# Low weight parts by ScalarE and an accumulating DMA in place of a VectorE subtraction: a decoder layer in split fp32 on one core

## The chip, the cores and the metric

The kernel runs on one core of one Trainium2 chip. The metric is the device time of one execution in microseconds (us). Five engines work side by side, each through its own queue in order: TensorE (PE in the profile, PEld its weight loads), VectorE (DVE), ScalarE (ACT), GpSimd (POOL) and SyncE (SP). SP issues nearly all DMAs of this kernel; 16 DMA engines carry them.

## The reference

One step of a decoder trunk with one layer, for a prompt of 1024 tokens and 8 sample tokens (1032 columns in all), width 1024, everything in fp32:

```
h   = rms_norm(x);  q, k, v, u, gates = split(h @ w_in)            # w_in: 1024 x 6400
a   = attention(q, k, v) @ w_attn_out                              # 3 groups of 4 heads, windows 128/512/2048
c   = swish(layer_norm(conv31(glu(u)))) @ w_conv_out
x  += rms_norm((sig(g0) * a + sig(g1) * c) @ w_out)
x  += rms_norm((silu(g) * up) @ w_ffn_out),  g, up = split(rms_norm(x) @ w_ffn_in)
x  += sigmoid(rms_norm(x) @ w_ple_gate) * (p @ w_ple_proj)
```

Besides x the kernel returns the new rows of the key/value caches and of the convolution's state.

## The kernel before

**Products in three passes.** Each fp32 operand is split into a high part in the type fp32r and a low part, the rest. A product of two split operands takes three matmuls: high by high, low activation by high weight, high activation by low weight. `mm3` issues them in this order; its three lines are L256, L257 and L258 in the profile. So L258 is the one that reads a weight's low part.

**Weights.** A weight tile is 128 partitions by 1024 fp32 (512 KB). `wq` lists 106 plain ones and 38 others in the order of use. `load_weight` loads a tile by a DMA on SP into one of `NRAW` = 3 buffers called `raw`. `ensure(i)` sees to it that the plain weights up to i are split: ScalarE copies `raw` into `wh` (high part, rounded to fp32r), VectorE subtracts, `wl = raw - wh`. The 38 weights of the first feed forward product from hidden tile 3 on go through `fetch` and `prepare` (Strassen's form, tiles `wah`, `wbh` ...) instead. `wh` and `wl` are slots of a pool of 43 that all large tiles share, so a new `wh` or `wl` may first wait until the last reader of its slot is done.

**Stages** (us of the profiled span): `w_in` with the depthwise convolution and the attention beside it, to about 520; branch gates with the combination of the attention groups and the layer norm of the convolution, to 690; the projection of branch A (`wi_A`), then of the convolution (`wi_C`, three weights held at a time), to 803; the output projection (`wi_O`, eight weights at once, by quarters of the tokens, `o_bank`), to about 895; the feed forward's first product (three plain hidden tiles, then Strassen's form), to 1355; its second product (`w_ffn_out`) in groups of hidden tiles, to 1609; the last gate (`wi_P`, `p_bank`) with the projection of p (`wi_pp`), to the end.

**Order.** The kernel is emitted in program order, but a scheduler moves instructions within each engine's queue by its own estimate of when each can run, except in `first_pairs`, where the order is pinned. A tile that is written or read in another way is thus not only produced differently: instructions around it on PE, ACT, DVE and POOL can change places too.

**GpSimd** before the change does 20 small powers, `r1 = r0 ** -0.5` in `token_rstd`, which give each norm's factors, and a few fills at the start. All engines' calls go through a wrapper, so that most lines of the profile on ACT, DVE and POOL read L116; one goes by the tiles' names.

Of the kernel before, what the change touches and what calls it, by code (L numbers as in the profile page):

```python
# [10 lines left out]
F32 = mybir.dt.float32  # L11
F32R = mybir.dt.float32r
AF = mybir.ActivationFunctionType
# [13 lines left out]
# token chunks; the last holds 256 prompt tokens and the 8 sample tokens  # L27
# [4 lines left out]
NRAW = 3  # L32
BUD = 2.95
# [3 lines left out]
# token chunks of the parts after the mix  # L37
# [17 lines left out]
def decoder_step(ctx: ExitStack, tc: tile.TileContext, ins, outs):  # L55
# [50 lines left out]
    class Engine:  # L106
        """An engine; its instructions stay in the order of emission while pinned[0] holds."""
# [59 lines left out]
    wq = []          # weight requests in the order of use: (dram view [128, n, 128], n)  # L167
# [21 lines left out]
    def fetch(j):  # L189
        """The next weight as it comes."""  # L190
        assert w_emitted[1] == j
        while w_emitted[0] < min(j + NRAW, len(wq)):
            load_weight()
        w_emitted[1] += 1
        return raws.pop(j)

    def ensure(i):
        """Weights up to i are loaded and split, the next ones on their way."""
        i = min(i, len(wq) - 1)
        while w_emitted[1] <= i:  # L200
            while w_emitted[0] < min(w_emitted[1] + NRAW, len(wq)):
                load_weight()
            j = w_emitted[1]
            r, n = raws.pop(j), wq[j][1]
            hi, lo = act("wh", F32R), act("wl", F32R)
            A.activation(hi[:, :n * P], r[:, :n * P], AF.Copy)
            V.tensor_sub(lo[:, :n * P], r[:, :n * P], hi[:, :n * P].bitcast(F32))
            wt[j] = tuple(x[:, :n * P].rearrange("p (k m) -> p k m", m=P) for x in (hi, lo))
            w_emitted[1] += 1
# [8 lines left out]
    def pump(us):  # L218
        """Background work of about so many microseconds of VectorE."""
        credit[0] += us  # L220
        while credit[0] > 0 and bg:
            try:
                credit[0] -= next(bg[0]) or 1.0
            except StopIteration:
                bg.popleft()
        if not bg:
            credit[0] = 0
# [3 lines left out]
    def tick(us):  # L231
        """Once per bank of `us` microseconds: the first chain goes on as far as VectorE's share allows."""
        if chains:
            ch = chains[0]
            ch[1] += us * RATE
            while ch[1] > 0:
                try:
                    ch[1] -= next(ch[0])
                except StopIteration:
                    chains.popleft()  # L240
                    break

    def finish(key):
        """The chains up to the one named."""
        while any(ch[2] == key for ch in chains):
            tick(5)
# [4 lines left out]
    def rng(c):  # L251
        """The token range of a chunk: its number among CH, or the range itself."""
# [7 lines left out]
    def gemm_bank(wi, xs, c, nk=KT, mid=None):  # L260
        """One bank: 128 output features by the tokens of chunk c."""
# [13 lines left out]
    def gemm_bank_rows(wis, f, xs, c):  # L275
        """One bank, the weights held by rows: wis[k] has all output features of k."""
# [19 lines left out]
    def token_rstd(acc, c):  # L296
        """acc: SBUF [128, chunk] -> rstd columns of the tokens from the sums over the partitions."""
# [22 lines left out]
    class SumSq:  # L320
        """Sum of squares over feature tiles."""
# [25 lines left out]
    def split_scaled(src, g, hi, lo, c):  # L347
        """src * g per feature -> hi and lo."""
# [5 lines left out]
    def chunk_slots(name):  # L354
        """Four slots that hold a chunk of eight feature tiles, and the tiles' views."""
# [9 lines left out]
    # =====================================================================  # L365
    # weight order
    # =====================================================================
# [19 lines left out]
    # feed forward: the first tiles as they are, then pairs of gate and up  # L387
# [13 lines left out]
    # =====================================================================  # L401
    # start: loads, transposes, first norm, pp = p @ w_ple_proj
    # =====================================================================
# [44 lines left out]
    def setup():  # L448
# [25 lines left out]
        # relative position biases: table values by distance, as rows for skewed reads and as columns  # L474
# [41 lines left out]
        # biases of the sample's slots: the first 13 by distance, the tokens' own in every 16th row  # L516
# [143 lines left out]
    def qkv_out(i):  # L660
        """The rows of the sample's tokens."""
# [12 lines left out]
    def kv_prompt_out(g, hp, dst, srcT):  # L674
        """The prompt's last rows, features by positions in the group's order."""
# [215 lines left out]
    # =====================================================================  # L891
    # phase 1: u / q, k, v with convolution and attention beside them
    # =====================================================================
# [56 lines left out]
    def first_pairs():  # L950
        """The first norm and the first two pairs, chunk by chunk.

        The products of the chunks 0 and 1 start before the factors of the tokens are known; they come in
        with the banks' results, and the chunks' operands are made again with them.
        """
# [86 lines left out]

# [27 lines left out]
    # branch gates  # L1070
# [12 lines left out]
    # =====================================================================  # L1083
    # branch A's projection; swish of the convolution; branch B; merge
    # =====================================================================
# [24 lines left out]
    def blocks(wis, fn, per, nc_=3):  # L1110
        """Blocks of `per` weight tiles held on chip, the chunks outermost inside a block."""
# [26 lines left out]
    def residual_norm(c, mv, rb, v_post, d_res, sq2, per):  # L1138
        """mv(f) (f32) -> residual + its norm in place, tile by tile; the sums of squares into sq2."""
# [13 lines left out]
    # =====================================================================  # L1153
    # output projection, by quarters of the tokens; norms up to the feed forward
    # =====================================================================
    # the mix as f32: halves of the tokens, two feature tiles to a slot
# [24 lines left out]
    # Strassen's form of the products with w_ffn_in (Winograd's variant): sums of the operands' quarters  # L1181
    tsum = [[None] * 4 for _ in range(2)]

    def token_sums(p):
        """The sums of the quarters of h2 for the tokens of half p: T1 = B12 - B11, T2 = B22 - T1,
        T3 = B22 - B12, T4 = B21 - T2, as hi and lo, four feature tiles to a slot."""
# [31 lines left out]
    def cache_copies():  # L1218
        """The caches move up by one row."""
# [13 lines left out]
    # =====================================================================  # L1233
    # feed forward, first product: hidden tiles into DRAM
    # =====================================================================
# [15 lines left out]
    def prepare(j):  # L1251
        """Gate's and up's weights of hidden tile j (A11, A12; A21, A22: tiles by halves of the features):
        S1 = A21 + A22, S2 = S1 - A11, S3 = A11 - A21, S4 = A12 - S2, as hi and lo."""
# [112 lines left out]
    # =====================================================================  # L1366
    # feed forward, second product, in groups of hidden tiles
    # =====================================================================
# [29 lines left out]
    # the last norm's operand, by chunks: three feature tiles to a slot  # L1398
    hp = [None] * 3

    def last_chain(ci, sq):
        """Residual and norm; the last norm's operand without the factors of the tokens, these into rbs."""
# [19 lines left out]
    for ci, c in enumerate(LC):  # L1422
# [7 lines left out]
        if nf < KT:  # L1430
            # the last banks side by side: the operands are done with one after the other
# [16 lines left out]
    # =====================================================================  # L1448
    # per-layer embedding gate and the outputs
    # =====================================================================  # L1450
# [87 lines left out]
def _lay_out(x):  # L1538
    """The inputs as the chip reads them: features by tokens, weights by tiles."""
# [17 lines left out]
def _rows(k, v, g):  # L1557
    """[2, 128 features, positions] of K and V -> [rows, 2, 4, 64] in the order of time."""
# [32 lines left out]
```

## Time and profile before

| | |
|---|---|
| Time, median of two runs | 1735.7 us (1734.86 to 1736.55) |
| Span of the profiled execution, first to last instruction | 1731.0 us |
| TensorE busy (matmul) | 1712.0 us, 99% |
| TensorE busy (weight loads) | 1661.9 us, 96% |
| VectorE busy | 1220.9 us, 71% |
| ScalarE busy | 620.9 us, 36% |
| GpSimd busy | 21.5 us, 1% |
| DMA | 171.47 MB, packets 29.8% of 16 engines' time on SP's queue |

The page gives the profiled execution's span and not a time of its own with what lies around the span; the two runs lie 3.9 to 5.6 us above that span, their median 4.7. A busy PE is one with a matmul in flight: matmuls overlap, so its share tells how little it idled, not how near it is to its peak.

### The profile page before, as it was taken

The page shows a single profiled execution, that of the slowest core. Times are in us where ns is not written, and L with a number is a line of the kernel's source. Part 1 is how long each engine was busy: PE and PEld are TensorE (multiplying, and loading weights), DVE is VectorE, ACT ScalarE, POOL GpSimd, SP SyncE. Part 2 cuts the span into 40 slices and gives each one's busy share as a digit, 9 for nine tenths or more (in the row PEclk, how much of TensorE's full clock was granted, in tenths as well). Part 3 has the DMA queues.
Part 4 walks back from the last instruction along what each step waited for, and adds up shares of the span by engine and source line. Part 5 has one row for each costly group of instructions (what it writes and reads, how often), then busy time and mean ns, then how long its engine had stood idle before and what let it go on. Part 6 is the DMA issues. An engine that isn't in the chain of part 4 may idle for free.

```text
span 1731.0 us, 29699 instructions
## 1 busy us (share of the span) xinstructions
PE 1712.0 (99%) x12086; PEld 1661.9 (96%) x12086; DVE 1220.9 (71%) x2188; ACT 620.9 (36%) x1303; POOL 21.5 (1%) x29
## 2 busy tenths in 40 slices
PE   7999999999999999999999999999999999999999
PEld 7999998999989999999999999999999999999998
DVE  7899779858969696744577866666666545637863
ACT  6434434444352254323354432233332311213530
POOL 0000000000000000000000000000000000000000
PEclk9999999999999999999999999999999999999999
DMA  5231121121343322622252232233333532520411
GB/s 188 65 121 65 43 66 44 60 75 41 112 156 103 123 95 96 203 80 85 80 163 70 74 98 94 86 98 98 110 98 116 188 138 90 181 94 13 148 58 45
DMA packets 82254, 171.47 MB, mean 99 GB/s; under 512 B 11026, under 2 KB 52034, under 8 KB 81734
## 3 DMA queue, kind: packets, MB, share of 16 engines
q1 hardware_dynamic: 82118, 169.58, 29.8%
q8 instruction: 94, 1.54, 0.4%
q14 instruction: 42, 0.34, 0.1%
HBM read 133.04 MB, written 50.01 MB: 106 GB/s over the span
## 4 chain that ended last, share of the span: by engine, by line
PE 96%; DVE 2%; issue 1%; POOL 0%; DMA 0%; ACT 0%; POOLq 0%; SPq 0%; DVEq 0%
PE g L256 30%; PE g L258 30%; PE g L257 30%; PE S L592 1%; PE O L630 1%; PE PT L615 1%; DVE ogl L116 1%; PE m L317 0%; PE m L300 0%; PE m L690 0%; POOL r L116 0%; DVE acc L116 0%; DMA raw<-in_w_in_dram 0%; PE m L876 0%; DVE cs L116 0%
## 5 line engine op out<-in xcount | busy, mean ns | idle before, releaser
L256 PE MATMUL g<-hh,wh 128*128 128x384 f32 (+1 forms) x1200 | 393.3, 328 | 7.0 <-ACT wh L116 7.0
L257 PE MATMUL g<-hl,wh 128*128 128x384 f32 (+1 forms) x1200 | 386.6, 322 | 0.0
L258 PE MATMUL g<-hh,wl 128*128 128x384 f32 (+1 forms) x1200 | 386.3, 322 | 0.3 <-DVE wl L116 0.3
L116 DVE SCALAR_TENSOR_TENSOR y<-z,taps,y 128x1023 f32<-128x1023 f32 (+14 forms) x240 | 304.2, 1267 | 31.7 <-ACT y L116 26.1
L256 PEld LDWEIGHTS g<-hh,wh 128*128 128x128 f32 x1200 | 227.2, 189 | 10.7 <-ACT wh L116 7.0
L258 PEld LDWEIGHTS g<-hh,wl 128*128 128x128 f32 x1200 | 226.8, 189 | 1.5 <-DVE wl L116 0.8
L257 PEld LDWEIGHTS g<-hl,wh 128*128 128x128 f32 x1200 | 227.3, 189 | 0.9
L257 PE MATMUL g<-ul,wh 128*128 128x344 f32 x528 | 168.9, 320 | 0.0
L258 PE MATMUL g<-uh,wl 128*128 128x344 f32 x528 | 168.7, 320 | 0.0
L256 PE MATMUL g<-uh,wh 128*128 128x344 f32 x528 | 162.8, 320 | 0.6 <-DVE fa L116 0.6
L116 DVE TENSOR_TENSOR wl<-raw,wh 128x1024 fp32r<-128x1024 f32 x106 | 128.9, 1220 | 22.9 <-ACT wh L116 19.9
L116 DVE TENSOR_TENSOR pk<-pk,g 128x258 f32<-128x258 f32 x266 | 105.3, 420 | 52.4 <-PE g L258 36.9
L256 PE MATMUL g<-mh,wh 128*128 128x258 f32 x448 | 127.2, 285 | 0.0
L258 PE MATMUL g<-mh,wl 128*128 128x258 f32 x448 | 126.6, 283 | 0.0
L257 PE MATMUL g<-ml,wh 128*128 128x258 f32 x448 | 126.5, 283 | 0.0
L116 ACT ACTIVATE wh<-raw 128x1024 fp32r<-128x1024 f32 x106 | 110.7, 1052 | 6.5 <-DMA raw<-in_w_in_dram 4.2
L116 DVE TENSOR_TENSOR fa<-fa,g 128x344 f32<-128x344 f32 x96 | 47.1, 511 | 76.9 <-PE g L258 76.5
L258 PEld LDWEIGHTS g<-uh,wl 128*128 128x128 f32 x528 | 99.2, 188 | 0.0
L257 PEld LDWEIGHTS g<-ul,wh 128*128 128x128 f32 x528 | 99.2, 188 | 0.0
L256 PEld LDWEIGHTS g<-uh,wh 128*128 128x128 f32 x528 | 98.1, 188 | 0.9 <-DVE fa L116 0.9
L256 PE MATMUL g<-th,wbh 128*128 128x258 f32 x304 | 86.0, 283 | 0.0
L258 PE MATMUL g<-mh,wal 128*128 128x258 f32 x304 | 86.0, 283 | 0.0
(246 smaller groups left out, 3840.3 us busy)
## 6 DMA issues: line engine op xcount, KB each, us to landing
raw<-in_w_in_dram SPq DMA_DIRECT2D x50, 512.0 KB
raw<-in_w_ffn_in_dram SPq DMA_DIRECT2D x44, 512.0 KB
hr<-d_h SPq DMA_DIRECT2D x22, 516.0 KB
raw<-in_w_ffn_out_dram SPq DMA_DIRECT2D x22, 512.0 KB
d_h<-pk SPq DMA_DIRECT2D x38, 258.0 KB
out_kvs_dram<-in_cache_kv_w_dram SPq DMA_DIRECT2D x16, 510.0 KB
res<-in_xT_dram SPq DMA_DIRECT2D x8, 516.0 KB
d_x<-mo SPq DMA_DIRECT2D x32, 129.0 KB
```

Of the source, the lines that this page charges most:

```text
L116: ins = fn(*a, **k)
L256: TE.matmul(ps, hi_w, xh, start=first, stop=False)
L257: TE.matmul(ps, hi_w, xl, start=False, stop=False)
L258: TE.matmul(ps, lo_w, xh, start=False, stop=last)
L592: TE.matmul(sp[h][:, ko:256], qT[h * 64:(h + 1) * 64, blk * P:(blk + 1) * P], kT[h * 64:(h + 1) * 64, k0:k0 + nk], start=True, stop=True)
L615: TE.transpose(ps[:, o:o + P], e[:, o:o + P], ident)
L630: TE.matmul(ps[h * 64:(h + 1) * 64, :P], vtok[:, (blk - 1 + kb) * P + h * 64:(blk - 1 + kb) * P + (h + 1) * 64], p[:, (h * 2 + kb) * P:(h ...
```

## The change

`ensure` makes the low part in another way for every plain weight but the first four. ScalarE writes the negated high part into `wl` (the same rounding, with a factor of -1), and a DMA issued from GpSimd adds `raw` to it in place. The subtraction on VectorE goes.

```
+FIRST = 4
 ...
     def ensure(i):
         ...
             r, n = raws.pop(j), wq[j][1]
             hi, lo = act("wh", F32R), act("wl", F32R)
             A.activation(hi[:, :n * P], r[:, :n * P], AF.Copy)
-            V.tensor_sub(lo[:, :n * P], r[:, :n * P], hi[:, :n * P].bitcast(F32))
+            if j < FIRST:
+                V.tensor_sub(lo[:, :n * P], r[:, :n * P], hi[:, :n * P].bitcast(F32))
+            else:
+                A.activation(lo[:, :n * P], r[:, :n * P], AF.Copy, scale=-1.0)
+                G.dma_start(lo[:, :n * P].bitcast(F32), r[:, :n * P], accum_op=ALU.add)
             wt[j] = tuple(x[:, :n * P].rearrange("p (k m) -> p k m", m=P) for x in (hi, lo))
```

Counted in the built programs: 102 subtractions leave VectorE, 102 passes of 128x1024 come to ScalarE, 102 DMAs of 512 KB to GpSimd's queue. Three places show how the queues stand. Lines shift with the change: L256 to L258 become L262 to L264.

**ScalarE at the start of the output projection**, before (`mo` is a bank's result, `sq` and `acc` its squares for the norm, `wh` the high part of the next weight):

```order
L116 ACTIVATE mo_7947<-g_7955 128x258
L116 ACTIVATE wh_7985<-raw_7745 128x1024
L116 ACTIVATE acc_7981<-mo_7947 128x258
L116 ACTIVATE wh_8020<-raw_7941 128x1024
L116 ACTIVATE mo_7947<-g_7989 128x258
L116 ACTIVATE sq_8015<-mo_7947 128x258
L116 ACTIVATE mo_7948<-g_8024 128x258
L116 ACTIVATE wh_8055<-raw_7983 128x1024
```

and now:

```order
L117 ACTIVATE mo_8005<-g_8013 128x258
L117 ACTIVATE wh_8043<-raw_7801 128x1024
L117 ACTIVATE acc_8039<-mo_8005 128x258
L117 ACTIVATE wl_8044<-raw_7801 128x1024
L117 ACTIVATE wh_8079<-raw_7998 128x1024
L117 ACTIVATE mo_8005<-g_8048 128x258
L117 ACTIVATE wl_8080<-raw_7998 128x1024
L117 ACTIVATE sq_8074<-mo_8005 128x258
L117 ACTIVATE mo_8006<-g_8084 128x258
```

Each weight now has two passes there, and they stand between the banks' evacuations.

**TensorE in the same stage**, where the bank of the fifth of the eight weights begins, before:

```order
L256 MATMUL g_8094<-mh_7139,wh_8055 128x258
L257 MATMUL g_8094<-ml_7140,wh_8055 128x258
L258 MATMUL g_8094<-mh_7139,wl_8056 128x258
L256 MATMUL g_8094<-mh_7178,wh_8055 128x258
L257 MATMUL g_8094<-ml_7179,wh_8055 128x258
```

and now at the matching place:

```order
L264 MATMUL g_8120<-mh_7841,wl_8080 128x258
L262 MATMUL g_8156<-mh_7189,wh_8115 128x258
L263 MATMUL g_8156<-ml_7190,wh_8115 128x258
L262 MATMUL g_8326<-mh_7189,wh_8000 128x258
L263 MATMUL g_8326<-ml_7190,wh_8000 128x258
L264 MATMUL g_8326<-mh_7189,wl_8001 128x258
L262 MATMUL g_8326<-mh_7229,wh_8000 128x258
```

Between the bank's first two matmuls and the one that needs the new low part, `wl_8116`, the scheduler has put a whole bank (`g_8326`) of a weight that is already there, for a later quarter of the tokens. It has done so once more for the seventh weight (`g_8286`, ahead of the first use of `wl_8188`).

**GpSimd in the last gate**, before:

```order
L116 TENSOR_TENSOR r_2283_16857<-r_2282_16855,mhalf 128x3
L116 TENSOR_TENSOR r_2293_16920<-r_2292_16918,mhalf 128x3
L116 TENSOR_TENSOR r_2359_17308<-r_2358_17306,mhalf 128x3
L116 TENSOR_TENSOR r_2368_17364<-r_2367_17362,mhalf 128x3
L116 TENSOR_TENSOR r_2401_17574<-r_2400_17572,mhalf 128x3
```

and now:

```order
L117 DMA wl_17189<-raw_17141 128x1024
L117 DMA wl_17303<-raw_17167 128x1024
L117 TENSOR_TENSOR r_2359_17406<-r_2358_17404,mhalf 128x3
L117 DMA wl_17350<-raw_17186 128x1024
L117 TENSOR_TENSOR r_2368_17462<-r_2367_17460,mhalf 128x3
L117 DMA wl_17357<-raw_17300 128x1024
L117 TENSOR_TENSOR r_2401_17672<-r_2400_17670,mhalf 128x3
```

The powers of the norms now stand in one queue with the DMAs, behind whichever was put ahead of them.

## The prediction

> **What bounds the kernel now.** First the busy shares and the chain of work that ended last, then PE's list of waits.
>
> ```profile
> PE 1712.0 (99%) x12086; PEld 1661.9 (96%) x12086; DVE 1220.9 (71%) x2188; ACT 620.9 (36%) x1303; POOL 21.5 (1%) x29
> PE 96%; DVE 2%; issue 1%; POOL 0%; DMA 0%; ACT 0%; POOLq 0%; SPq 0%; DVEq 0%
> PE g L256 <- ACT wh L116: 7.0, 1, 7.0
> PE m L317 <- POOL r L116: 5.0, 6, 1.6
> ...
> PE g L256 <- DVE fa L116: 0.6, 1, 0.6
> ...
> PE g L258 <- DVE wl L116: 0.3, 1, 0.3
> ```
>
> TensorE sets the time: it is 96% of the chain and idles 19.0 us of 1731.0. The largest wait, 7.0 us, is the start, where the pinned first weights keep their subtraction. PE waited for a low part on VectorE only once, for 0.3 us. So a VectorE that has less to do has almost nothing to give: the 0.6, the 0.3 and at best the 5.0 us for the norms' powers, some 6 us in all. What the change can cost has no such limit, since each low part must be there before its first L258.
>
> **What is taken away and put in its place.**
>
> ```profile
> L116 DVE TENSOR_TENSOR wl<-raw,wh 128x1024 fp32r<-128x1024 f32 x106 | 128.9, 1220 | 22.9 <-ACT wh L116 19.9
> L116 ACT ACTIVATE wh<-raw 128x1024 fp32r<-128x1024 f32 x106 | 110.7, 1052 | 6.5 <-DMA raw<-in_w_in_dram 4.2
> L116 POOL TENSOR_TENSOR r<-r,mhalf 128x3 f32<-128x3 f32 x20 | 19.2, 962 | 1624.4 <-DVE cs L116 972.1 <-DVE r L116 622.2 <-PE g L258 30.1
> 254.75 0.37 SPq L116 DMA_DIRECT2D raw<-in_w_in_dram  x1
> DMA  0000000000009843975799979799640000000000
> ```
>
> 102 of the 106 subtractions go: 102 x 1.22 = 124 us off VectorE, 1221 to about 1096. ScalarE gets 102 passes of the shape of `wh`: 102 x 1.05 = 107 us, 621 to about 728 (42%). Neither is on the chain as an average. What counts is each weight's way: before, 1.22 us after the high part; now 1.05 us of ScalarE, then the DMA.
>
> The trace has no accumulating DMA and none from GpSimd, so its time D (issue to landing) is bounded. The nearest row is a weight's load of the same 512 KB, alone: issued at 254.75; in the window from 254.5 with slices of 0.1 us the DMA engines start in the 13th slice and end in the 30th, 255.7 to 257.5: 1.0 us of lead, 1.8 of transfer, taken as 2.0 with the completion. **Lower end, 3.0 us**: the accumulation moves like that load. **Value taken, 6.0 us**: it reads two tiles for each that it writes, so twice the transfer, 4.0; the lead of 1.0; and 1.0 for GpSimd to issue it, by the 0.96 us of its only regular instruction, the power. **Upper end, 10.0 us**: the transfer four times as long, 8.0. I take the middle value because the second read is certain, and nothing speaks for more.
>
> The Trainium skill (DMA: Bandwidth & Descriptors, Anatomy of one DMA — SWDGE (gpsimd) path) gives a fit for GpSimd's DMAs, about 2.0 us plus bytes over 436 GB/s; for 512 KB an estimate by it is 3.2 us, near the lower end, though its fit is for plain transfers. By that figure the sum below would be 11.7 us in place of 57.3.
>
> **The sum.** A low part is now ready 1.05 + D = 7.05 us after its high part is done. In most places the weight is made 15 to 20 us ahead and nothing waits. These are the places where it is not; the first row of each pair is the weight's high part (in the third pair the old subtraction), the second the first matmul that needs the low part.
>
> ```profile
> 592.52 1.05 ACT L116 ACTIVATE wh<-raw 128x1024 fp32r<-128x1024 f32 x1
> 596.99 0.34 PE L258 MATMUL g<-hh,wl 128*128 128x384 f32 x1
> 621.18 1.05 ACT L116 ACTIVATE wh<-raw 128x1024 fp32r<-128x1024 f32 x1
> 627.72 0.34 PE L258 MATMUL g<-hh,wl 128*128 128x384 f32 x1
> 714.40 1.22 DVE L116 TENSOR_TENSOR wl<-raw,wh 128x1024 fp32r<-128x1024 f32 x1
> 716.82 0.34 PE L258 MATMUL g<-sh,wl 128*128 128x384 f32 x1
> 718.35 1.04 ACT L116 ACTIVATE wh<-raw 128x1024 fp32r<-128x1024 f32 x1
> 721.04 0.34 PE L258 MATMUL g<-sh,wl 128*128 128x384 f32 x1
> 806.26 1.05 ACT L116 ACTIVATE wh<-raw 128x1024 fp32r<-128x1024 f32 x1
> 808.90 0.28 PE L258 MATMUL g<-mh,wl 128*128 128x258 f32 x1
> 812.04 1.05 ACT L116 ACTIVATE wh<-raw 128x1024 fp32r<-128x1024 f32 x1
> 814.71 0.28 PE L258 MATMUL g<-mh,wl 128*128 128x258 f32 x1
> 817.83 1.05 ACT L116 ACTIVATE wh<-raw 128x1024 fp32r<-128x1024 f32 x1
> 820.50 0.28 PE L258 MATMUL g<-mh,wl 128*128 128x258 f32 x1
> 943.74 1.05 ACT L116 ACTIVATE wh<-raw 128x1024 fp32r<-128x1024 f32 x1
> 949.14 0.28 PE L258 MATMUL g<-mh,wl 128*128 128x258 f32 x1
> 1604.79 2.00 ACT L116 ACTIVATE wh<-raw 128x1024 fp32r<-128x1024 f32 x2
> 1609.37 0.32 PE L258 MATMUL g<-ph,wl 128*128 128x344 f32 x1
> 1618.08 1.04 ACT L116 ACTIVATE wh<-raw 128x1024 fp32r<-128x1024 f32 x1
> 1621.24 0.43 PE L258 MATMUL g<-ph,wl 128*128 128x344 f32 x1
> 1627.01 2.00 ACT L116 ACTIVATE wh<-raw 128x1024 fp32r<-128x1024 f32 x2
> 1631.30 0.32 PE L258 MATMUL g<-pTh,wl 128*128 128x344 f32 x1
> ```
>
> - Branch gates: 592.52 + 1.05 + 7.05 = 600.62 against 596.99, a wait of 3.6; the next, 629.28 against 627.72, 1.6.
> - Convolution's projection: the low part's slot is there at 714.40 at the latest, so 721.45 against 716.82, 4.6; then 726.44 against 721.04, 5.4.
> - Output projection: eight weights are held, their slots come free in pairs as PE ends with the old ones, and PE is 2.7 us behind each time. The first pair: 814.36 against 808.90, 5.5. The second and third would be 5.4 each, but the order now puts a bank of a weight already there ahead of each: 814.71 - 808.90 = 5.81 us for two banks, 2.9 each, so 2.5 and 2.5 stay.
> - Feed forward, third plain hidden tile: 951.84 against 949.14, 2.7.
> - Last gate: 1612.89 against 1609.37, 3.5; 1626.17 against 1621.24, 4.9; 1635.11 against 1631.30, 3.8. At the middle one the scheduler has also put two sigmoids between the two passes.
>
> Together 40.6 us. I add them up, since each wait moves PE and with it the release of the next slots.
>
> Second, the buffers. A `raw` buffer is now held until the DMA has read it: load 3.0, two passes 2.1, DMA 6.0, 11.1 us for three buffers, 3.7 per weight. In the output projection PE takes a new one every 2.9: six weights x 0.8 = 4.8 us. Elsewhere a weight has over 10 us, and this is hidden.
>
> Third, the clock.
>
> ```profile
> 525.00:528.60 3.60, 2.61 (x19) 2.33 (x18) 3.60 (x6) 0.18 (x1) 0.00 (x0) 1.00 0.39 124
> 528.60:532.00 3.40, 3.40 (x14) 3.40 (x13) 3.40 (x5) 0.91 (x2) 0.00 (x0) 0.50 0.21 81
> ```
>
> The windows (the eighth number is the granted clock) show PE busy 2.61 of 3.60 us, and the clock at half for the 3.4 us behind it, which loses 1.7 us of work. Seven of the waits above are at least 3.4 us: 7 x 1.7 = 11.9.
>
> The Trainium skill (TensorE: Matmul & The Clock Gate, Part 1: The HAM clock gate) has the clock halve after a whole idle window of about 3.4 us. The row speaks against waiting for a whole one: 0.99 us of idling with some tiny matmuls was enough here. By the row's rule the waits of 2.5 and 2.7 us would pay too, 3 x 1.7 = 5.1 us more than by the page's.
>
> Sum: 40.6 + 4.8 + 11.9 = 57.3 us on the span of 1731.0; with the 4.7 between span and median, **1793 us**.
>
> **The ends.** With D = 3.0 the same places give 0.6, 0, 1.6, 2.4, 2.5, 0, 0, 0, 0.5, 1.9, 0.8 = 10.3, no loss by buffers (8.1 / 3 = 2.7) and none by the clock: 1746. With D = 10.0 each wait is 4.0 longer, 84.6; buffers (15.1 / 3 - 2.9) x 6 = 13.2; clock 11 x 1.7 = 18.7: 116.5, so 1852.
>
> **Rivals.**
> - *The DMA is nearly as quick as a load* (D below 4.5): 1746 to about 1769. For it: SBUF is both source and target, and the DMA engines stand at 29.8% of their time on SP's queue. Against it: the second read. Chance 0.29.
> - *The scheduler covers it: not slower.* The order shows that it knows of the wait: two banks were moved ahead in the output projection. If it does so at all eleven places with 2.9 us each, and D is 3.0, no wait is left, and VectorE's relief gives back up to 6 us: 1730 to 1736. It decides from D + 1.05 below about 4. Against it: outside the output projection the banks share one weight's low part, and there is little to move. Chance 0.06, a third of it for more than 2% faster in ways I don't see; the idle time of 19.0 us is 1.1% and allows none.
> - *Throughput*: the accumulation is slow in the DMA engines themselves, above 8 us of them per tile. Then loads queue behind it, and with them `hr`, `res` and the raw weights: 1852 and more. 102 x 8 = 816 us of 1731 beside the 29.8%: not full, but full in the second product and the last gate. Chance 0.17.
> - *GpSimd's queue*: in the last gate powers stand behind DMAs that wait for ScalarE. PE waits for the powers six times already, 5.0 us. If each of three late ones waits another 3 us, that is 9 us on top, within the range; no case of its own.
>
> **Chances and range.** Forecast (D from 4.5 to 8, about 1769 to 1830): 0.48. With the rivals: slower by over 2% (above 1770.4, about what a measurement of this kernel can tell from no change) 0.64, within it 0.34, faster 0.02. The range is 1744 to 1852: it takes in the quick DMA and leaves out the cover and most of the throughput case.
>
> **What would show it.** PE's waits: L264 waiting for a DMA `wl` in place of VectorE, some 40 us in about eleven pieces, most at 593, 717 to 722, 809 to 825 and 1609 to 1632 of the old time, each shift added. VectorE near 1096, ScalarE near 728 us busy. The DMA's time from GpSimd's issue to the last packet: 6 us is right, 3 or 10 decides between the rivals. The clock below 1.0 in the windows behind the long waits. Wrong would be: waits in the attention stage, where 15 us of lead should hide all, or PE waiting for ScalarE's evacuations rather than for low parts.

## The result, and the profile after

The changed kernel takes **1796.2 us** (two runs, 1792.58 and 1799.79) against 1735.7: 1.0355 times as long, 95% interval 1.0298 to 1.0413. The total is 3 us from the forecast. What makes it up is not what was forecast.

The page of the changed kernel (busy times; the queue of GpSimd's DMAs with packets, MB and share of 16 engines' time; a line of the costliest groups, with the mean time of one in ns; the DMA issues, whose last number is the median time from issue to landing):

```profile
PE 1736.9 (97%) x12086; PEld 1679.7 (93%) x12086; DVE 1112.1 (62%) x2086; ACT 712.0 (40%) x1405; POOL 108.8 (6%) x131
...
q0 software_dynamic: 14688, 53.48, 16.0%
...
L117 POOL DMA_DIRECT2D wl<-raw x102 | 88.8, 871 | 1418.4 <-ACT wl L117 816.8
...
wl<-raw POOLq DMA_DIRECT2D x102, 512.0 KB, 5.5
```

VectorE is relieved as planned, and TensorE waits more. Its list of waits, and the core's mean granted clock:

```profile
PE g L264 <- DMA wl<-raw: 15.0, 11, 3.4
PE g L262 <- ACT uh L117: 10.2, 3, 4.8
PE g L262 <- ACT wh L117: 7.5, 2, 7.0
PE m L306 <- DVE acc L117: 7.1, 4, 6.2
PE m L323 <- POOL r L117: 6.6, 9, 1.3
PE m L465 <- DMA strow<-in_state_conv_dram: 4.8, 1, 4.8
PE g L262 <- ACT pk L117: 2.2, 1, 2.2
```

```profile
core 0: 1797.7 us, clock 0.985
```

TensorE idles 1797.7 - 1736.9 = 60.8 us, 41.8 more than before. The clock lost 0.015 x 1797.7 = 27.0 us (before, at 0.999, 1.7), 25.3 more. 41.8 + 25.3 = 67.1, against 66.7 us between the two spans: the account closes. But low parts (`wl`) are only 15.0 of the 41.8. More than that falls on `uh` (the high part of a hidden tile, second product), `acc` (a norm's sum of squares, 6.9 more than before) and `strow` (the cached convolution state, loaded in the attention stage): 21.9 us for three things that the change doesn't touch.

How `uh` comes to be late is to be seen in the second product. The timeline (start, duration, operation, in brackets the idle time before) on GpSimd, SP, ScalarE and TensorE:

```profile
1386.54 0.86 POOL L117 DMA_DIRECT2D wl<-raw  x1 [7.73 <-ACT wl L117]
...
1395.20 0.33 SPq L117 DMA_DIRECT2D raw<-in_w_ffn_out_dram  x1
1395.63 0.38 SPq L117 DMA_DIRECT2D hr<-d_h  x1
...
1400.85 1.06 ACT L117 ACTIVATE uh<-hr 128x1032 fp32r<-128x1032 f32 x1 [1.69 <-DMA hr<-d_h]
...
1413.04 1.23 PE L262 MATMUL g<-uh,wh 128*128 128x344 f32 x3 [4.82 <-ACT uh L117]
```

and that one DMA of GpSimd among the issues of its window:

```profile
wl<-raw POOLq DMA_DIRECT2D x1, 512.0 KB, 8.6
```

Issued at 1386.54, it lands 8.6 us later, at 1395.2. Until then it holds its `raw` buffer. At 1395.20 SP, whose queue is in order, issues the load that waited for that buffer, and at 1395.63 the load of the hidden tile `hr` behind it, which ScalarE then awaits. The next round ends with TensorE waiting 4.8 us for `uh`.

### The profile page after: what moved, and what is told of

It is laid out like the page before. It is cut to its first block, busy times and chain, and to the rows that moved or that the text cites. A ratio compares the mean times of both kernels' runs of the same rounds, so it can differ in the third digit from the quotient of the medians.

```text
span 1797.7 us, 30018 instructions
## 1 busy us (share of the span) xinstructions
PE 1736.9 (97%) x12086; PEld 1679.7 (93%) x12086; DVE 1112.1 (62%) x2086; ACT 712.0 (40%) x1405; POOL 108.8 (6%) x131
## 4 chain that ended last, share of the span: by engine, by line
PE 87%; DMA 5%; issue 4%; ACT 2%; DVE 2%; POOL 1%; SPq 0%; POOLq 0%; ACTq 0%; DVEq 0%
PE g L262 27%; PE g L264 27%; PE g L263 27%; DMA wl<-raw 2%; PE S L598 1%; PE O L636 1%; PE PT L621 1%; DMA hr<-d_h 1%; ACT wl L117 1%; PE m L323 0%; DMA raw<-in_w_ple_gate_dram 0%; POOL r L117 0%; ACT wh L117 0%; PE m L882 0%; DVE ogl L117 0%
## 5 line engine op out<-in xcount | busy, mean ns | idle before, releaser
L262 PE MATMUL g<-hh,wh 128*128 128x384 f32 (+1 forms) x1200 | 395.4, 329 | 7.0 <-ACT wh L117 7.0
L264 PE MATMUL g<-hh,wl 128*128 128x384 f32 (+1 forms) x1200 | 388.9, 324 | 0.3 <-DVE wl L117 0.3
L263 PE MATMUL g<-hl,wh 128*128 128x384 f32 (+1 forms) x1200 | 388.6, 324 | 0.0
L262 PEld LDWEIGHTS g<-hh,wh 128*128 128x128 f32 x1200 | 228.9, 191 | 10.3 <-ACT wh L117 7.0
L264 PEld LDWEIGHTS g<-hh,wl 128*128 128x128 f32 x1200 | 228.5, 190 | 1.8 <-DVE wl L117 0.8
L263 PEld LDWEIGHTS g<-hl,wh 128*128 128x128 f32 x1200 | 228.8, 191 | 1.1
L262 PE MATMUL g<-uh,wh 128*128 128x344 f32 x528 | 165.7, 326 | 13.0 <-ACT uh L117 10.2
L117 POOL DMA_DIRECT2D wl<-raw x102 | 88.8, 871 | 1418.4 <-ACT wl L117 816.8
L264 PE MATMUL g<-uh,wl 128*128 128x344 f32 x528 | 170.6, 324 | 0.1
L263 PE MATMUL g<-ul,wh 128*128 128x344 f32 x528 | 170.4, 324 | 0.0
L264 PE MATMUL g<-mh,wl 128*128 128x258 f32 x448 | 127.7, 288 | 8.3 <-DMA wl<-raw 8.1
L262 PE MATMUL g<-mh,wh 128*128 128x258 f32 x448 | 128.1, 289 | 0.5 <-ACT wh L117 0.5
L263 PE MATMUL g<-ml,wh 128*128 128x258 f32 x448 | 127.7, 287 | 0.0
L262 PEld LDWEIGHTS g<-uh,wh 128*128 128x128 f32 x528 | 100.0, 192 | 14.6 <-ACT uh L117 11.2
L117 ACT ACTIVATE wl<-raw 128x1024 fp32r<-128x1024 f32 x102 | 107.1, 1050 | 14.4 <-DVE sl L117 7.5
L264 PEld LDWEIGHTS g<-uh,wl 128*128 128x128 f32 x528 | 101.0, 191 | 0.4 <-DMA wl<-raw 0.4
L263 PEld LDWEIGHTS g<-ul,wh 128*128 128x128 f32 x528 | 101.1, 192 | 0.0
L117 DVE TENSOR_TENSOR acc<-acc,sq 128x258 f32<-128x258 f32 (+3 forms) x137 | 62.8, 475 | 58.0 <-ACT sq L117 56.6
```

The source lines that it names most:

```text
L117: ins = fn(*a, **k)
L262: TE.matmul(ps, hi_w, xh, start=first, stop=False)
L263: TE.matmul(ps, hi_w, xl, start=False, stop=False)
L264: TE.matmul(ps, lo_w, xh, start=False, stop=last)
```

## Experiments

Four explanations stood against each other: late low parts, as forecast (**latency**); the `raw` buffer held until the DMA lands, with whatever queues behind the next load (**hold**); the extra work of the DMA engines (**traffic**); ScalarE's second pass (**ScalarE**). All runs, with PE's waits of the profiled one in us; the clock's loss is (1 - mean clock) x span, good to about 0.9 us, since the clock is given to three places:

| run | time | ratio to before (95%) | idle | wl by DMA | uh | acc | r | strow | clock's loss |
|---|---|---|---|---|---|---|---|---|---|
| before | 1735.7 | | 19.0 | 0 | 0 | 0.2 | 5.0 | 0 | 1.7 |
| changed | 1796.2 | 1.0355 (1.0298-1.0413) | 60.8 | 15.0 | 10.2 | 7.1 | 6.6 | 4.8 | 27.0 |
| scalar_vector | 1734.4 | 1.0005 (0.9995-1.0016) | 20.0 | 0 | 0 | 0 | 4.3 | 0 | 1.7 |
| sub_store | 1736.2 | 1.0011 (1.0000-1.0022) | 21.2 | 0 | 0 | 0.7 | 4.8 | 0.7 | 5.2 |
| dead_add | 1785.7 | 1.0289 (1.0273-1.0305) | 51.6 | 0 | 13.8 | 7.6 | 3.8 | 3.4 | 21.4 |
| wh_source | 1818.6 | 1.0494 (1.0473-1.0514) | 78.5 | 45.6 | 0 | 7.9 | 6.7 | 3.9 | 32.7 |
| short_add | 1754.9 | 1.0107 (1.0090-1.0124) | 29.8 | 3.6 | 3.6 | 1.1 | 7.1 | 0 | 10.5 |
| attn_only | 1740.4 | 1.0029 (1.0020-1.0039) | 23.5 | 0 | 0 | 0.2 | 5.0 | 3.6 | 0 |
| raw4 | 1793.5 | 1.0345 (1.0329-1.0362) | 56.8 | 18.1 | 2.5 | 6.9 | 6.1 | 3.9 | 21.5 |
| b_raw4 | 1735.5 | 1.0005 (0.9991-1.0018) | 19.9 | 0 | 0 | 0.2 | 5.0 | 0 | 3.5 |
| hr_pool | 1785.9 | 1.0308 (1.0286-1.0330) | 54.1 | 21.8 | 0.5 | 6.7 | 6.6 | 4.0 | 16.0 |
| traffic_only | 1773.8 | 1.0237 (1.0205-1.0268) | 51.9 | 0 | 3.1 | 0.2 | 29.2 | 3.1 | 26.7 |
| dead_raw4 | 1782.4 | 1.0279 (1.0264-1.0294) | 50.8 | 0 | 11.9 | 12.7 | 3.8 | 3.0 | 21.4 |
| dead_pre3 | 1778.8 | 1.0241 (1.0217-1.0264) | 48.7 | 0 | 10.2 | 12.3 | 3.2 | 3.8 | 21.3 |

In every run the scheduler orders the queues anew, so a few us between two runs can be order alone.

**ScalarE's pass alone** (scalar_vector).

```
-                G.dma_start(lo[:, :n * P].bitcast(F32), r[:, :n * P], accum_op=ALU.add)
+                V.tensor_add(lo[:, :n * P], r[:, :n * P], lo[:, :n * P].bitcast(F32))
```

> ScalarE's negated pass stays, but VectorE adds raw to it in place of the DMA (102 additions of about 1.2 us, so VectorE near 1220, ScalarE near 715 us). ScalarE theory (the second pass in ScalarE's queue delays evacuations and hidden tiles): 1760 us or more. Hold, latency and traffic theories: 1735 to 1745, the low part only some 1 us later than in the kernel before, PE idle near 20 us.

```profile
PE 1710.9 (99%) x12086; PEld 1659.7 (96%) x12086; DVE 1221.9 (71%) x2188; ACT 712.4 (41%) x1405; POOL 21.8 (1%) x29
```

ScalarE is as busy as in the changed kernel, and the time is that of before. The pass costs nothing; the ScalarE theory is out, and all 60 us come from the DMA.

**The DMA without a waiting low part** (dead_add).

```
-                A.activation(lo[:, :n * P], r[:, :n * P], AF.Copy, scale=-1.0)
-                G.dma_start(lo[:, :n * P].bitcast(F32), r[:, :n * P], accum_op=ALU.add)
+                V.tensor_sub(lo[:, :n * P], r[:, :n * P], hi[:, :n * P].bitcast(F32))
+                G.dma_start(r[:, :n * P], hi[:, :n * P].bitcast(F32), accum_op=ALU.add)
```

> VectorE's subtraction makes the low part as before, and ScalarE's second pass goes; GpSimd's accumulating DMA of 512 KB stays for each of the 102 weights, but it adds wh to the raw buffer that nothing reads any more. So the DMA engines' work, GpSimd's issue and the hold of raw stay, and no low part waits. Latency theory: 1735 to 1742 us, PE idle near 20 us. Hold and traffic theories: 1760 us or more, with PE's waits for uh, acc and strow as in the changed kernel (22 us) and none for wl.

```profile
PE g L262 <- ACT uh L117: 13.8, 5, 4.1
...
PE m L306 <- DVE acc L117: 7.6, 4, 3.5
...
PE m L465 <- DMA strow<-in_state_conv_dram: 3.4, 1, 3.4
```

With no low part that depends on it, the DMA still costs 51 of the 60 us. Latency as the sole cause is refuted: the waits for `uh`, `acc` and `strow` appear without it, 24.8 us in sum against 22.1 in the changed kernel.

**The same bytes by a plain DMA** (sub_store).

```
-                A.activation(lo[:, :n * P], r[:, :n * P], AF.Copy, scale=-1.0)
-                G.dma_start(lo[:, :n * P].bitcast(F32), r[:, :n * P], accum_op=ALU.add)
+                V.tensor_sub(lo[:, :n * P], r[:, :n * P], hi[:, :n * P].bitcast(F32))
+                G.dma_start(d_junk[j % 8], r)
```

> VectorE's subtraction stays, and GpSimd issues for each of the 102 weights a dead plain DMA of raw into DRAM (512 KB read, 512 KB written): raw is held until it has read, the DMA engines have more to do, but no low part waits for it. Hold theory: about 1765 to 1775 us (1736 + 36), with waits for uh, acc and strow and none for wl. Latency theory: 1736 to 1742. Traffic theory: at least half of the 60 us, 1765 and more; it is told from the hold by the run in which the DMA adds wh.

Its queue, its group and its issues:

```profile
q0 software_dynamic: 14688, 53.48, 7.9%
...
L117 POOL DMA_DIRECT2D d_junk<-raw x102 | 55.0, 539 | 1378.3 <-DMA raw<-in_w_ffn_out_dram 566.5
...
d_junk<-raw POOLq DMA_DIRECT2D x102, 512.0 KB, 3.9
```

Packets and bytes are equal to the number, but the time in the DMA engines is half (7.9% against 16.0%), the landing 3.9 us against 5.5, and the cost 1.8 us (3.8 at the upper end of the interval). So 512 KB more per weight is not enough for the loss, and the traffic theory, as I had sized it, missed.

The hold was not put to the test, though the run was made for that too. The plain DMA reads `raw` alone, so it waits only for the load (the group's line) and need not wait for ScalarE or VectorE. SP's waits show it, first the changed kernel, then this run:

```profile
SPq L117 <- DMA wl<-raw: 633.0, 96, 36.5
```

```profile
SPq L117 <- DVE wl L117: 463.5, 79, 34.6
...
SPq L117 <- DMA d_junk<-raw: 50.1, 8, 20.4
```

In the changed kernel SP waits 96 times for an accumulation, here 79 times for VectorE's subtraction, as before the change, and only 8 times for the dead DMA. One such DMA is issued at 437.76 us, as soon as its weight's load has landed, and is through 2.9 us later; SP's next load, at 445.84, comes with the end of a subtraction. So the accumulation differs from this DMA in two things: it takes longer, and it can only begin when the passes before it are done.

**An eighth of the accumulation** (short_add).

```
-                G.dma_start(lo[:, :n * P].bitcast(F32), r[:, :n * P], accum_op=ALU.add)
+                G.dma_start(lo[:, :P].bitcast(F32), r[:, :P], accum_op=ALU.add)
```

> The accumulating DMA adds only the first 128 of a weight's 1024 columns (64 KB); the other low parts stay the negated high part and are wrong. Both ScalarE passes, the issue on GpSimd, the order and all waits stay. Theory that the time goes with the DMA's length (reading and adding 512 KB, longer when a load runs beside it): issue to landing near 2.5 to 3 us, so by the sum of the prediction for 3.0 us about 1746 (1738 to 1752). Theory that the fixed part of such a DMA or the queues' order sets the cost: 1770 us or more.

```profile
wl<-raw POOLq DMA_DIRECT2D x102, 64.0 KB, 2.4
```

1754.9 us, between the two expectations: two thirds of the loss go with the DMA's length. With the length both the hold and the DMA engines' work shrink, so the run doesn't tell these two apart. The 64 KB still take 2.4 us, and about 20 us of loss stay with them (idle 10.8 more than before, clock 8.8).

**The buffer freed, the latency kept** (wh_source).

```
-                G.dma_start(lo[:, :n * P].bitcast(F32), r[:, :n * P], accum_op=ALU.add)
+                G.dma_start(lo[:, :n * P].bitcast(F32), hi[:, :n * P].bitcast(F32), accum_op=ALU.add)
```

> The accumulating DMA adds the high part wh instead of raw, so the low parts come out as zero (the low weight's share of every product with these 102 weights is left out); the DMA, its size, its queue and PE's wait for it stay, but a raw buffer is free after ScalarE's two passes and no longer held until the DMA lands. Hold theory (the loads and passes queued behind a held raw buffer cost the waits for uh 10.2, acc 7.1 and strow 4.8 us, and the half clock behind them some 13): about 1760 us (1750 to 1770), these three waits near zero, the waits for wl still near 15. Latency theory (all comes from low parts that are late): 1796 as the changed kernel. Traffic theory (512 KB more per weight in the DMA engines): 1796.

All three theories missed: the run is 22 us slower than the changed kernel. `uh` is at zero, as hold had it, but `acc` (7.9) and `strow` (3.9) stay, and the waits for `wl` rise to 45.6. For `acc` the trace shows another cause here: ScalarE waits 7.3 us until a store (`d_gA<-sg`) has landed. For `wl` the issues show why, in the window from 100 to 520 us, in the changed kernel:

```profile
wl<-raw POOLq DMA_DIRECT2D x29, 512.0 KB, 4.6
```

and with the buffer freed:

```profile
wl<-wh POOLq DMA_DIRECT2D x29, 512.0 KB, 5.9
```

with its SP and GpSimd in the timeline:

```profile
438.03 0.36 SPq L117 DMA_DIRECT2D raw<-in_w_in_dram  x1
...
438.30 0.87 POOL L117 DMA_DIRECT2D wl<-wh  x1 [15.69 <-ACT wl L117]
```

The next load now starts 0.3 us before the accumulation instead of behind its landing (in the changed kernel that load is issued 4.6 us after the accumulation), and both are under way at once. No low part is waited for in this stage. In the second product, where 13.6 of the 45.6 us are, the median landing goes from 6.2 to 9.3 us, and over the whole kernel from 5.5 to 7.3. Holding the buffer is thus not only a cost: it keeps that load out of the accumulation's way.

**A fourth raw buffer** (raw4, and its control b_raw4).

```
-NSLOT = 43
-NRAW = 3
+NSLOT = 42
+NRAW = 4
```

> The changed kernel with four raw buffers in place of three, paid with one of the 43 large slots (its control, the kernel before with the same sizes, is run next). Hold theory: a load then waits for a DMA that was issued a weight earlier, so most of the waits for uh, acc and strow go: 1755 to 1775 us. Latency theory: 1796 or a little more, for the slot that is missing. Traffic theory: 1796.

> Control for the run with four raw buffers: the kernel before with NRAW = 4 and NSLOT = 42. If the missing slot costs nothing: 1733 to 1737 us, and the 4 us that the fourth buffer gave the changed kernel are its whole gain. If the missing slot costs, that much more of a gain by the buffer was hidden: 1745 us and more would leave the hold theory alive.

The control is the time of before: the missing slot is free. The fourth buffer gains 3 us, not 20 to 40, and the two runs of the changed kernel lie 7 us apart, so even the 3 are not sure. The waits for `uh` do fall, from 10.2 to 2.5, but those for `wl` rise by 3.1 and those for `pk` by 2.8. The hold theory was wrong to count on slack: whatever the number of buffers, the load that `ensure` asks for at a weight takes the buffer of the weight just before it, so it waits for the DMA issued last, and stands ahead of that weight's `hr`.

**Hidden tiles past SP's queue** (hr_pool).

```
-        SY.dma_start(r, d_h[j])
+        G.dma_start(r, d_h[j])
```

> The changed kernel, but the loads of the hidden tiles (hr, second product, 22 of 512 KB) are issued by GpSimd, so they no longer stand behind a raw load on SP that waits for a buffer. Theory of SP's queue: the waits for uh (10.2 us) and the half clock behind them go: about 1780 us (1775 to 1787), with PE's wait for uh below 3 us. Traffic theory: hr still lands late beside the accumulating DMAs, or the low parts do instead: 1790 to 1800 us.

```profile
PE g L264 <- DMA wl<-raw: 21.8, 15, 3.4
...
PE g L262 <- ACT uh L117: 0.5, 1, 0.5
```

1785.9: the waits for `uh` are gone as SP's queue had it, and 6.8 us come back as low parts, as traffic had it. The intervals of the two ratios still touch; the stage itself is plainer. The first and last start of the 528 matmuls `g<-uh,wh` of the second product, in before, the changed kernel, hr_pool and dead_add, in this order:

```profile
L256 PE MATMUL g<-uh,wh x528: 313/319/423, 1355.4 to 1608.6; 128*128 128x344 f32 x176
```

```profile
L262 PE MATMUL g<-uh,wh x528: 313/319/656, 1396.1 to 1666.0; 128*128 128x344 f32 x176
```

```profile
L262 PE MATMUL g<-uh,wh x528: 313/319/424, 1389.7 to 1651.9; 128*128 128x344 f32 x176
```

```profile
L262 PE MATMUL g<-uh,wh x528: 313/320/655, 1378.9 to 1657.1; 128*128 128x344 f32 x176
```

253.2, 269.9, 262.2 and 278.2 us: the stage lost 16.7 by the change and 9.0 with `hr` on the other queue. The dead DMA lost 25.0 there; why more than the change itself is open. That `hr` loads more slowly is not the reason: where ScalarE waited for it, the time from its issue to the start of `uh` is 4.8 us in the median with the dead DMA and 4.7 before (6.0 in the changed kernel).

**Traffic without hold or latency** (traffic_only).

```
-                A.activation(lo[:, :n * P], r[:, :n * P], AF.Copy, scale=-1.0)
-                G.dma_start(lo[:, :n * P].bitcast(F32), r[:, :n * P], accum_op=ALU.add)
+                V.tensor_sub(lo[:, :n * P], r[:, :n * P], hi[:, :n * P].bitcast(F32))
+                G.dma_start(junk[:, :n * P], hi[:, :n * P].bitcast(F32), accum_op=ALU.add)
```

> VectorE's subtraction stays; for each of the 102 weights GpSimd's accumulating DMA of 512 KB adds wh to a tile of its own that nothing reads (one of the 43 large slots pays for it, and each such DMA waits for the one before). So the DMA engines have the same extra work, but raw is free as early as in the kernel before, and no low part waits. Hold theory (the dead DMA cost 51 us since it kept raw, and loads stood behind the load that waited for it): 1735 to 1745 us. Traffic theory (loads, stores and copies are slower beside it): 1765 us or more, with waits for uh, acc and strow as with the dead DMA into raw.

Its largest wait, its GpSimd, and its matmuls of the second product:

```profile
PE m L325 <- POOL r L117: 29.2, 10, 9.0
```

```profile
859.50 0.86 POOL L117 DMA_DIRECT2D junk<-wh  x1 [4.15 <-DMA junk<-wh]
860.07 1.20 POOL L117 TENSOR_TENSOR r<-r,mhalf 128x3 f32<-128x3 f32 x1
```

```profile
L264 PE MATMUL g<-uh,wh x528: 313/320/652, 1389.5 to 1647.9; 128*128 128x344 f32 x176
```

The 39 us say little by themselves (and the profiled run is the slowest of four, 1783.0): the one junk tile made a new bound. 33 of the DMAs wait on GpSimd for the one before, the norms' powers stand behind, and PE waits 24 us more for those. In the second product, where few powers stand, the stage takes 258.4 us: by this run bare traffic costs some 5 us there, of the 17 to 25 that change and dead DMA lose.

**The dead DMA with four buffers, asked for four or three ahead** (dead_raw4, dead_pre3).

```
-NSLOT = 43
-NRAW = 3
+NSLOT = 42
+NRAW = 4
+AHEAD = 3        # dead_pre3 alone: in fetch and ensure, in place of NRAW
```

> The run with the dead accumulating DMA into raw (1785.7 us), with NRAW = 4 and NSLOT = 42, whose control was 1735.5. Hold theory: the fourth buffer takes up a DMA of 4.5 to 6 us, since a weight's turn is at least 7 us in most stages, so 1740 to 1755 us. Traffic theory: within 10 us of 1785.

> The run with the dead accumulating DMA into raw and four raw buffers (1782.4 us), but only three weights are asked for ahead, as with three buffers: the load issued at a weight's turn then takes the buffer of the weight before the last, not that of the last, whose DMA has only just been issued. The DMA engines' work is the same. Theory of SP's queue (the load at its head waits until the last accumulating DMA has landed, with hr, strow and the stores behind it): 1738 to 1752 us, of which some 10 are the bare traffic, by the run with a junk tile less its waits for the powers; uh, acc and strow below 8 us in sum. Traffic theory: 1770 us or more.

Where the hold theory had 1740 to 1755, dead_raw4 is the same as the dead DMA with three buffers within the intervals, and dead_pre3 is some 8 us faster by the ratios. dead_raw4 follows from raw4: the load still takes the buffer of the weight just before. dead_pre3 did not do what it was made for: the scheduler put the loads back ahead of `hr` in SP's queue. Its SP's waits, and its SP in the timeline:

```profile
SPq L118 <- DMA raw<-wh: 563.6, 92, 31.2
```

```profile
1528.29 0.33 SPq L118 DMA_DIRECT2D raw<-in_w_ffn_out_dram  x1
1528.67 0.42 SPq L118 DMA_DIRECT2D hr<-d_h  x1
```

SP waits for dead DMAs 92 times: the load at 1528.29 comes right after the landing of the one issued last, at 1521.33 (6.9 us), and `hr` still stands behind it. So this run decides nothing between SP's queue and traffic.

**The attention stage alone** (attn_only).

```
-            if j < FIRST:
+            if j < FIRST or j >= 34:
```

> The changed form for 30 of the 102 weights alone, those of w_in up to the end of the convolution and the attention; the other weights keep the subtraction. Theory of tight places: only the wait at the load of strow and the half clock behind it are left, 5 to 6 us: 1738 to 1743 us. Theory of a cost per DMA (60 us / 102 each): 18 us, 1752.

30 of the 102 DMAs cost 5.5 us, not the 18 of an equal share. The one new wait of size is `strow`, 3.6 us, in a profiled run that is the fastest of ten (1736.1); no low part from a DMA is waited for. The loss sits at places, not in each DMA.

**What is shown, and what is open.** Shown: the DMA costs it all, and ScalarE's pass nothing; late low parts are not needed for most of it; the bytes alone, by a plain DMA that is done early, cost next to nothing; two thirds go with the accumulation's length; SP's order accounts for the waits for `uh`. Three ways of paying stand in for one another: hold the buffer, and loads come late; free it, and low parts come late; move a load to GpSimd, and part of its gain returns as low parts. Open: how the 51 us of the dead DMA divide between the accumulation's load on the DMA engines and the held buffer outside the second product. The plain DMA did not hold the buffer, the junk tile made a queue of its own on GpSimd, and with three weights asked for ahead SP's order came back. Open too is what makes `acc` and `strow` late, since both waits stay with the buffer freed. No version beat the kernel before.

## Why the prediction was right in its sum and wrong in its parts

- **VectorE's relief is worth nothing; the cost is in waits on TensorE: right.** VectorE came to 1112 for 1096, ScalarE to 712 for 728.
- **D = 6.0 us: near, in part by luck.** The 6.0 was worked out for a DMA alone, and alone it takes 4.5 to 4.6; the median is 5.5 because loads run beside many. The doubled transfer fits: 0.160 x 1797.7 / 102 = 2.8 us of all 16 engines per DMA, against 0.079 x 1736.0 / 102 = 1.3 for the plain one; that the second read makes the difference was not tried. I also took D as a constant; in the second product single ones took 8.6 and 10.5 us.
- **Low parts, 40.6 us: wrong, 15.0.** By stretches of PE's waits in the changed kernel: convolution's projection, output projection, third plain hidden tile, last gate.

```profile
PE g L264 <- DMA wl<-raw: 0.9, 1, 0.9
...
PE g L264 <- DMA wl<-raw: 6.3, 4, 3.4
...
PE g L264 <- DMA wl<-raw: 1.9, 1, 1.9
...
PE g L264 <- DMA wl<-raw: 6.0, 5, 2.0
```

  Against 10.0, 10.5 (15.3 with the buffers), 2.7 and 12.2; the gates' 5.2 never came. The hidden tile came near. In the convolution's projection the step that failed is "the low part's slot is there at 714.40 at the latest": that was when VectorE got to the second weight's low part, and I used an upper bound as the value. Now ScalarE writes that weight's low part here, and the accumulation and the first use follow:

```profile
730.55 1.06 ACT L117 ACTIVATE wl<-raw 128x1024 fp32r<-128x1024 f32 x1 [7.47 <-DVE sl L117]
731.91 0.86 POOL L117 DMA_DIRECT2D wl<-raw  x1 [8.88 <-ACT wl L117]
738.83 0.45 PE L264 MATMUL g<-sh,wl 128*128 128x384 f32 x1 [0.89 <-DMA wl<-raw]
```

  The pass begins 7.4 us before TensorE is ready for the low part (738.83 - 0.89 - 730.55), where I had 2.4 (716.82 - 714.40); pass, issue and landing take 8.3, and 0.9 is left as the wait. At the gates the two weights also had more lead: from the start of the high part to the first use 8.0 us (599.00 to 606.98) and 10.3 (631.17 to 641.50), in place of 4.5 and 6.5, while the low part landed after 6.8 and 8.1. TensorE was by then 10 and 14 us behind its old times, ScalarE's passes 6.5 and 10. Why the last gate was over-sized no run shows.
- **The held buffer, 4.8 us, "elsewhere a weight has over 10 us, and this is hidden": wrong.** I counted how often a buffer comes round, and not what stands behind the waiting load on SP, nor behind its pass on ScalarE. 21.9 us of waits for `uh`, `acc` and `strow` came on top. For `uh` two runs show it (wh_source, hr_pool). For `acc` the trace of the changed kernel does, where ScalarE waits for a load and has the squares of the norm behind it:

```profile
660.26 1.06 ACT L117 ACTIVATE wh<-raw 128x1024 fp32r<-128x1024 f32 x1 [2.92 <-DMA raw<-in_w_attn_out_dram]
...
664.61 0.87 PE L306 MATMUL m<-ident,acc 128*128 128x128 f32 x3 [6.22 <-DVE acc L117]
```

  The load of `strow` is issued on SP at 67.00, behind a load of `raw` at 65.09. But with the buffer freed both waits stay, so that the hold alone makes them is not shown. Both signs that were named as "wrong would be" appeared: a wait in the attention stage (`strow`), and waits for ScalarE's tiles (`uh`, `pk`).
- **The clock, 11.9 us: wrong in size, 25.3.** I let each wait of 3.4 us or more cost 3.4 us at half clock. Windows of the changed kernel (PE busy first, the granted clock third from the end):

```profile
984.00:987.70 3.70, 1.85 (x14) 1.63 (x14) 2.34 (x7) 1.76 (x3) 0.86 (x1) 1.00 1.01 207
987.70:991.10 3.40, 3.40 (x18) 3.40 (x18) 0.00 (x0) 0.00 (x0) 0.00 (x0) 0.50 1.01 205
...
1411.00:1417.80 6.80, 4.76 (x17) 4.76 (x18) 2.61 (x4) 2.96 (x3) 0.86 (x1) 0.50 0.62 148
```

  A wait of 1.9 us was enough for one half-speed window, and at 1411 half speed lasted 6.8 us. Some 5 us of the 25.3 lie where no wait stands ahead (last section). The Trainium skill (TensorE: Matmul & The Clock Gate, Part 1: The HAM clock gate) lets the clock fall after a whole idle window of about 3.4 us; the first two rows speak against it, and for the dearer of the two readings that the prediction weighed.
- **The rivals.** The quick DMA did not happen. The cover did, in pieces and outside the output projection too: in the third plain hidden tile seven pairs of L262 and L263 now run ahead of the first L264 (983.60 to 987.41), where before each L258 followed its pair. Throughput was set at 8 us of the engines per tile, and 2.8 were measured; but what it described, loads and `hr` late, is what the hold did at that smaller size. GpSimd's queue cost 1.6 us more for `r`, within its 9; it is dear only in the run with the junk tile, 24 us.

That 1793 came so near is thus luck, two errors that cancel: 30.4 us too many in low parts and their buffers (45.4 against 15.0), and 40.2 too few in the other waits (26.8) and the clock (13.4). The 9.8 that are left on the span shrink to 3 us on the time, since the profiled run is the slower of the two, 3.6 us above their median, and lies 2.1 us above its span in place of the 4.7 that I added. In the prediction's sum for the upper end the buffers come to 12.8 us, not 13.2; the 1852 stays.

## What to carry over

A step that is moved to a DMA keeps its source as well as its result busy until it lands: ask which load waits for that source, and what stands behind this load in its in-order queue, before summing the waits for the result. Take the DMA's time with the loads beside it, not alone, since freeing the source early only moved the wait (1796 to 1819 us). Before a run with a dead DMA is read as "the buffer is held", see in the trace that a load waited for it. Spare time on an engine off the path, here VectorE's 30%, is no reason to pay for its relief.

## What the runs showed of the hardware

- An accumulating DMA of 512 KB inside SBUF took 2.1 times the engine time of a plain one of the same packets into DRAM (16.0% against 7.9%), 4.5 to 4.6 us to land alone and up to 10.5 beside loads, and 0.87 us of GpSimd to issue against 0.54. 64 KB of it still took 2.4 us.
- The clock also fell where TensorE had hardly idled. Beside the combination of the attention groups, whose matmuls of 16 rows stand among the gates':

```profile
602.00:605.40 3.40, 3.33 (x20) 2.48 (x19) 3.09 (x4) 0.39 (x1) 0.17 (x1) 1.00 0.82 157
605.40:615.60 10.20, 10.20 (x32) 8.91 (x32) 8.46 (x9) 1.06 (x1) 0.00 (x0) 0.50 0.59 220
```

  PE is busy 3.33 of 3.40 us, and half speed follows for 10.2. What sets it off there was not tried.
